# A two-layer encoder trunk on one core: the first weight matrix loaded raw from ScalarE's queue and split on the engines, and two low parts of the first quad computed on VectorE

## The chip, the cores and the metric

The kernel runs on one core of a Trainium2 chip. The metric is the time of one execution on the device, in microseconds (us). The engines are named as in the profile: PE is TensorE (PEld its weight load), DVE is VectorE, ACT is ScalarE, POOL is GpSimd, SP is SyncE. SP, ACT and POOL can issue DMA transfers; SP's and ACT's go through hardware queues, POOL's through a software queue, and all of them share the 16 DMA engines of the core.

## What is computed

Two layers of a bidirectional encoder over 512 tokens of width 1024, in float32. Cut to what matters here, with `P_A` a windowed attention and `P_B` a neighbourhood attention, each followed by a projection:

```python
for l in range(DEPTH):                       # DEPTH = 2
    h = rms_norm(x, attn_norm_g[l])
    z = h @ w_in[l]                          # q_a, k_a, v_a, q_b, k_b, v_b, gate_a, gate_b
    x = x + (sigmoid(ga) * P_A(qa, ka, va) + sigmoid(gb) * P_B(qb, kb, vb)) @ w_out[l]
    h = rms_norm(x, ffn_norm_g[l])
    x = x + (silu(h @ w_gate[l]) * (h @ w_up[l])) @ w_down[l]    # hidden width 2816
```

## The kernel before

**Products in two parts.** A float32 operand is written as a high part, which is the value rounded to the type float32r, and a low part, which is the rest. A product is three matmuls that add into one PSUM bank: high by high, high by low, low by high. So every operand needs both parts before its product can be finished. `mm` (line 619) is one matmul; `UNIT` (line 420) is the planner's time for three.

**Weights.** `slab` (line 442) plans one piece of a weight matrix, at most 128 x 1024 per part; `w_load` (line 503) and `w_low` (line 512) bring it in. The high part is a POOL transfer that rounds on its way. The low part takes two steps: ACT writes minus the high part into the buffer, and a second POOL transfer adds the float32 weights from memory onto it. So a slab is read from memory twice, and ACT's step waits for the first landing and the second transfer for ACT. A slab's two steps fall due `LEAD_H` = 23 and `LEAD_L` = 15 us of planned matmul time ahead of its use; where they fall due before the first matmul, they are issued at the first `tick`.

**The start.** `x_load` (line 641) brings in the input in eight chunks of 128 columns (256 KB each) on SP's queue. SP also issues the identity matrix and the two norm gains, between the first and the second chunk. POOL issues the high parts of the first three slabs and then nine loads of small tables. ACT runs one tiny copy, `warm`, first of all. Then `token_matmul` (line 816) computes the first 512 columns of `z`: four PSUM banks (one for 128 tokens each), eight chunks of the contraction, and so 4 x 3 = 12 matmuls a chunk, 96 in all. A slab holds two chunks of the weights. While it runs, `start` (line 1068) prepares the chunks of x: four PE transposes into one bank, on ACT the high part times the gain, on DVE a copy of the transposed chunk to `xT`, then on DVE the low part, on ACT the square, on DVE the running sum of squares (`acc`). The first half of this (`second` false) and the second half are issued apart, two chunks ahead of their use: chunks 0 and 1 ahead of the first matmul, and chunk k + 2 in the midst of chunk k and its neighbour. Once all squares are added, `Norm.chain` (line 772) has PE sum them over the partitions (the matmuls `at<-ones`), and DVE makes the reciprocal root.

**The feed-forward part.** Its first 256 hidden columns are plain pairs (`pair_matmul`, line 797). The other 2560 are five quads of 512. For a quad the matrix is cut into four blocks and Strassen-like sums of blocks are multiplied: seven products, in the order `ORDER` = (1, 5, 6, 2, 7, 3, 4). `Quad` (line 537) loads the blocks a11, a12, a21, a22 as float32 from SP's queue, and for each product makes the sum on DVE, in place in the blocks (`high`, line 559), the high part on ACT, and the low part (`low`, line 575). In all quads but the first of each layer's `w_gate`, the low part is one DVE subtraction. For that first quad `by_transfer` is true (line 491): `low_by_transfer` (line 532) has ACT write minus the high part, and a POOL transfer from SBUF to SBUF adds the source block onto it. The sums for products 6 and 3 overwrite blocks from which such a transfer reads: product 6 writes a11, the source of product 1; product 3 writes a12, the source of product 2. DVE must wait there for the transfer to have landed. `chain_x` (line 1360) makes the same seven operands from x, and `m_step` (line 1459) multiplies. After product 1, ACT copies its bank to a second one (`seed`, line 1479), onto which products 6, 7 and 4 add.

**The order of the work.** Each engine works in the order in which its instructions were issued. Steps with a due time come from a list (`at_pos`, `tick`); the others are chains (generators), which a planner steps when its own model of the engines' clocks says that their inputs are ready. A dry pass makes these choices and also places all buffers in two arenas by their lives; the second pass follows it. So a change in one place can shift choices and places elsewhere.

Of the kernel before, what the change touches and what calls it, by code (L numbers as in the profile page):

```python
# [19 lines left out]
P = 128  # L20
# [193 lines left out]
def trunk(ctx: ExitStack, tc: tile.TileContext, a: dict, out: bass.AP, lay: Layout):  # L214
# [285 lines left out]

    highs, lows, used = {}, {}, [0]

    def w_load(i):

        if i not in highs:
            n1, n2, src = plan[i]
            highs[i] = buf([n1, n2], F32R)
            for at, ap in src:
                n = ap.shape[1]
                GQ.dma_start(highs[i][:, :, at : at + n], ap.rearrange("(k p) n -> p k n", p=P))  # L510
# [26 lines left out]
    class Quad:  # L537
# [37 lines left out]
        def low(self, m):  # L575
            src, h = self.parts[m]
            lo = buf([4, 256], F32R)
            if self.by_transfer:
                low_by_transfer(lo, src, h)
            else:  # L580
                V.tensor_tensor(lo, src, h.bitcast(F32), ALU.subtract)
            self.parts[m] = h, lo
# [50 lines left out]
    G.memset(vec2, 0.0)  # L633
    G.memset(ones, 1.0)
    G.memset(magic, 0x5F3759DF)
    warm = cp.tile([P, 2], F32, tag="warm", name="warm")
    A.copy(warm, ones)
    xv = a["x"].rearrange("o (b p) d -> p (o b) d", p=P)
    xin = []

    def x_load(c):
        t = act().rearrange("p (b n) -> p b n", b=NB)
        Q.dma_start(t, xv[:, :, P * c : P * c + P])
        xin.append(t)


    x_load(0)
    Q.dma_start(ident, a["consts"][:, :P])
    for i, n in enumerate(("attn_norm_g", "ffn_norm_g")):
        Q.dma_start(vec[16 * i : 16 * i + 16], a[n].rearrange("l (k p) -> (l k) p", p=P))  # L650
    w_load(0)
    for c in range(1, KD):
        x_load(c)
        if c in (3, 5):
            w_load((0, 3, 5).index(c))
    GQ.dma_start(cst[:, P:], a["consts"][:, P:])
    for i, n in enumerate(("q_norm_b", "k_norm_b")):
        for h in range(2):
# [7 lines left out]
        GQ.dma_start(gqa[:, i], a[n].rearrange("l d -> (l d)").unsqueeze(0).to_broadcast([P, DEPTH * HD]))  # L666
    snk = cp.tile([P, DEPTH, 8], F32, tag="snk", name="snk")
    GQ.dma_start(snk, a["sink_a"].rearrange("l h -> (l h)").unsqueeze(0).to_broadcast([P, DEPTH * 8]))
    ps = at_bank()
    T.transpose(ps[:, :32], vec, ident[:32, :32])  # L670
    V.tensor_copy(vecT, ps[:, :32])
# [144 lines left out]
    def token_matmul(nrm, evac, begin=None):  # L816

        ps = [mm_bank() for _ in range(NB)]
        if begin is not None:
            begin(0, False)  # L820
            w_low(0)
            begin(0, True)
            begin(1, False)
            begin(1, True)
            tick(0.0)
        for k0 in range(0, KD, 2):
            wk = w_take()
# [3 lines left out]
            for i, (b, k) in enumerate(order):  # L831
                t = slice(P * b, P * b + P)
                kk = k0 + k
                hi, lo = wk[k]
                mm(ps[b], nrm.xh[kk][:, t], hi, kk == 0, False)
                mm(ps[b], nrm.xh[kk][:, t], lo, False, False)
                mm(ps[b], nrm.xl[kk][:, t], hi, False, kk == KD - 1)
                tick(UNIT)
                if kk == KD - 1:
                    evac(b, ps[b])  # L840
                if begin is not None and i in (0, 2, 4, 6) and k0 < KD - 2:
                    begin(k0 + 2 + i // 4, i % 4 == 2)
                yield UNIT


# [219 lines left out]

    norms = {}

    def start(nrm, k, second):

        if not second:  # L1070
            ps = at_bank()
            for b in range(NB):
                T.transpose(ps[:, P * b : P * b + P], xin[k][:, b, :], ident)
            A.activation(held(nrm.xh[k]), by_columns(ps), AF.Copy, scale=gain(0, k))
            V.tensor_copy(held(xT[k]), by_columns(ps))
            return
        V.scalar_tensor_tensor(nrm.xl[k], xT[k], gain(0, k), nrm.xh[k].bitcast(F32), ALU.mult, ALU.subtract)
        sq = act()
        A.activation(sq, xT[k], AF.Square)
# [512 lines left out]
```

## Time and profile before

| What | us |
|---|---|
| median of 3 runs | 1482.7 |
| the three runs | 1484.63, 1482.7, 1477.24 |
| the profiled execution's own time | 1478.58 |
| its span, first to last instruction | 1476.8 |
| PE busy in it | 1405.2 |
| DVE, ACT, POOL busy | 908.5, 713.9, 368.6 |

The profiled execution took 1478.58 us and its span is 1476.8, so 1.8 us lie outside the span. All positions below are us from the span's start. In a timeline a row is a group of neighbouring instructions of one kind: where it starts, how long the group lasts, engine, operation, output and inputs by their names in the program, shape, count, and in brackets the idle time of the engine ahead of it with what ended it. Almost all instructions carry line 308, which is the helper that records them, so they are told apart by names: `arena` is any buffer in SBUF, `at` and `mm` are PSUM banks. A wait row reads: who waited, for whom, us in all, how often, the longest.

### The profile page before, as it was taken

The numbers are of one execution on the slowest core, as the hardware profiler recorded it, in microseconds if no ns is written. First come the engines' busy times: TensorE is split into PE (matmuls) and PEld (weight loads), VectorE is DVE, ScalarE is ACT, GpSimd is POOL, SyncE is SP. The second block draws the span as 40 slices with busy tenths as digits, with TensorE's granted clock in tenths as the row PEclk, the third lists the DMA queues.
The fourth block names the chain that finished last, engine by engine and source line by source line (L and its number), as shares of the span: only waits on it lengthen the run. The fifth ranks groups of instructions, "written<-read, shape, count | busy, mean of one in ns | idle before, by whom it ended". The sixth has DMA issues, their size and how long they took to land.

```text
span 1476.8 us, 21019 instructions
## 1 busy us (share of the span) xinstructions
PE 1405.2 (95%) x8074; PEld 1230.7 (83%) x8074; DVE 908.5 (62%) x1743; ACT 713.9 (48%) x1200; POOL 368.6 (25%) x374
## 2 busy tenths in 40 slices
PE   5999989999969999999999999999997999999998
PEld 4778878888869999999987887788886899999997
DVE  3876768543747565575647868673437575575653
ACT  3476657543544343433545775574345444343431
POOL 4533222234221110201353322123332211101111
PEclk9999999999989999999999999899999899999999
DMA  9877778899975745645798679669997754836455
GB/s 228 164 145 137 145 128 150 153 191 241 174 150 119 174 115 143 158 100 117 154 189 168 125 132 158 124 122 183 209 242 130 160 124 122 190 83 168 115 100 114
DMA packets 211427, 223.18 MB, mean 151 GB/s; under 512 B 25964, under 2 KB 179744, under 8 KB 211328
## 3 DMA queue, kind: packets, MB, share of 16 engines
q0 software_dynamic: 159920, 167.23, 61.1%
q1 hardware_dynamic: 51408, 54.62, 13.3%
q8 instruction: 63, 1.03, 0.3%
q14 instruction: 36, 0.29, 0.1%
HBM read 207.13 MB, written 2.10 MB: 142 GB/s over the span
## 4 chain that ended last, share of the span: by engine, by line
PE 69%; DMA 9%; DVE 9%; issue 7%; ACT 4%; POOL 2%; DVEq 0%; POOLq 0%; ACTq 0%; SPq 0%
PE mm L308 50%; PE at L308 19%; DVE arena L308 6%; ACT arena L308 4%; DMA arena<-arena 3%; DMA arena<-in_w_out 2%; DVE sm L308 2%; POOL arena L308 2%; DMA arena<-in_w_gate 1%; DMA arena<-in_w_up 1%; DMA arena<-in_rel_bias_b 1%; DMA vec<-in_q_norm_b 1%; DMA arena<-in_w_in 0%; ACT L308 0%; DVE hf L308 0%
## 5 line engine op out<-in xcount | busy, mean ns | idle before, releaser
L308 PE MATMUL mm<-arena 128*128 128x512 f32 (+1 forms) x5568 | 1127.9, 358 | 32.0 <-ACT mm L308 24.9
L308 PEld LDWEIGHTS mm<-arena 128*128 128x128 f32 x5568 | 910.1, 191 | 161.7 <-ACT mm L308 25.3
L308 PE MATMUL at<-arena 128*128 128x256 f32 (+2 forms) x1952 | 309.4, 299 | 15.1 <-DMA arena<-arena 12.3
L308 ACT ACTIVATE arena<-arena 128x1024 fp32r<-128x1024 f32 (+3 forms) x280 | 235.9, 865 | 176.9 <-DMA arena<-in_w_down 62.2
L308 ACT CAST arena<-arena 128x1024 fp32r<-128x1024 f32 (+2 forms) x250 | 211.7, 864 | 224.0 <-DVE arena L308 219.5
L308 PEld LDWEIGHTS at<-arena 128*128 128x128 f32 x1952 | 268.7, 193 | 38.7 <-DMA arena<-arena 11.9
L308 DVE TENSOR_TENSOR arena<-arena,arena 128x1024 fp32r<-128x1024 f32 (+2 forms) x236 | 228.3, 981 | 57.3 <-ACT arena L308 57.1
L308 POOL DMA_DIRECT2D arena<-in_w_in x168 | 168.4, 1367 | 368.3 <-ACT arena L308 367.9
L308 DVE TENSOR_TENSOR arena<-arena,mm 128x512 f32<-128x512 f32 x144 | 98.8, 686 | 255.9 <-PE mm L308 255.8
L308 POOL DMA_DIRECT2D arena<-in_w_down x96 | 98.2, 1210 | 503.2 <-ACT arena L308 388.4
L308 DVE TENSOR_TENSOR arena<-arena 128x1024 f32<-128x1024 f32 (+3 forms) x196 | 158.8, 824 | 19.2 <-DMA arena<-arena 14.1
L308 DVE TENSOR_TENSOR arena<-at,arena 128x384 fp32r<-128x384 f32 (+4 forms) x206 | 114.1, 562 | 52.7 <-ACT arena L308 45.9
L308 ACT CAST arena<-at 128x384 fp32r<-128x384 f32 (+2 forms) x164 | 74.4, 459 | 117.5 <-PE at L308 105.1
L308 PE MATMUL at<-cst,arena 128*128 128x128 f32 x504 | 87.4, 280 | 11.8 <-DVE arena L308 7.9
L308 PEld LDWEIGHTS at<-cst,arena 128*128 128x128 f32 x504 | 64.5, 143 | 30.5 <-DVE arena L308 10.9
L308 ACT ACTIVATE arena<-arena,negm 128x256 f32<-128x256 f32 (+1 forms) x128 | 71.6, 561 | 13.1 <-DVE negm L308 12.7
L308 DVE TENSOR_TENSOR arena<-mm,arena 128x512 f32<-128x512 f32 x72 | 49.3, 687 | 45.8 <-PE mm L308 45.7
L308 ACT COPY arena<-at 64x512 f32<-64x512 f32 (+1 forms) x60 | 34.8, 581 | 64.8 <-PE at L308 64.3
L308 POOL DMA_DIRECT2D arena<-in_w_out x32 | 35.2, 1292 | 54.5 <-ACT arena L308 54.5
L308 DVE CUSTOM_DVE_ANT_0 arena<-at,arena 128x256 f32<-128x256 f32 (+1 forms) x64 | 31.0, 486 | 28.7 <-PE at L308 28.4
L308 DVE CUSTOM_DVE_ANT_0 arena<-at,cst,nsnk 128x256 f32<-128x256 f32 (+1 forms) x64 | 34.3, 546 | 16.3 <-PE at L308 15.9
L308 DVE TENSOR_SCALAR arena<-arena,sm 128x384 f32<-128x384 f32 (+1 forms) x97 | 34.0, 405 | 1.1
(70 smaller groups left out, 444.2 us busy)
## 6 DMA issues: line engine op xcount, KB each, us to landing
arena<-in_w_in POOLq DMA_DIRECT2D x104, 512.0 KB, 7.1
arena<-in_w_down POOLq DMA_DIRECT2D x80, 512.0 KB, 6.8
arena<-in_w_gate SPq DMA_DIRECT2D x20, 1024.0 KB, 6.7
arena<-in_w_up SPq DMA_DIRECT2D x20, 1024.0 KB, 5.2
arena<-in_w_in POOLq DMA_DIRECT2D x64, 256.0 KB, 6.2
arena<-in_w_out POOLq DMA_DIRECT2D x32, 512.0 KB, 8.0
arena<-in_w_proj_a POOLq DMA_DIRECT2D x16, 512.0 KB, 8.8
arena<-in_w_proj_b POOLq DMA_DIRECT2D x16, 512.0 KB, 6.5
```

The costliest lines, as they stand in the source:

```text
L308: f(*args, **kw)
```

## The change

At the start, x and the first matrix (the four slabs of the first 512 columns) come in another way. `first_load` loads a slab as float32 on ACT's hardware queue, once; the first slab in two transfers of one chunk each. `first_parts` makes the two parts of one chunk on the engines: ACT copies it to the high part (which rounds), DVE subtracts. The two gains move from SP's to ACT's queue, the identity goes ahead of x on SP's queue, and `warm` goes behind ACT's transfers. `start` is no longer in two halves: chunk 0 is prepared ahead of the first matmul, and chunk k + 1 after the first bank's three matmuls of chunk k, so one chunk ahead. The copy to `xT` moves from DVE to ACT. In the first quad of each layer, the low parts of products 1 and 2 become DVE subtractions again.

```diff
+    FIRST = KD // 2
+    raws = []
+
+    def first_load(i):
+
+        n1, n2, ((_, ap),) = plan[i]
+        raws.append(buf([n1, n2]))
+        ap = ap.rearrange("(k p) n -> p k n", p=P)
+        for k in ([slice(0, 1), slice(1, 2)] if i == 0 else [slice(0, 2)]):
+            AQ.dma_start(raws[i][:, k], ap[:, k])
+        highs[i], lows[i] = buf([n1, n2], F32R), buf([n1, n2], F32R)
+
+    def first_parts(k):
+        raw, h, lo = raws[k // 2][:, k % 2], highs[k // 2][:, k % 2], lows[k // 2][:, k % 2]
+        A.copy(h, raw)
+        V.tensor_tensor(lo, raw, h.bitcast(F32), ALU.subtract)
...
-            if self.by_transfer:
+            if self.by_transfer and m not in (1, 2):
                 low_by_transfer(lo, src, h)
             else:
                 V.tensor_tensor(lo, src, h.bitcast(F32), ALU.subtract)
...
-    warm = cp.tile([P, 2], F32, tag="warm", name="warm")
-    A.copy(warm, ones)
...
-    x_load(0)
     Q.dma_start(ident, a["consts"][:, :P])
     for i, n in enumerate(("attn_norm_g", "ffn_norm_g")):
-        Q.dma_start(vec[16 * i : 16 * i + 16], a[n].rearrange("l (k p) -> (l k) p", p=P))
-    w_load(0)
-    for c in range(1, KD):
+        AQ.dma_start(vec[16 * i : 16 * i + 16], a[n].rearrange("l (k p) -> (l k) p", p=P))
+    for c in range(KD):
         x_load(c)
-        if c in (3, 5):
-            w_load((0, 3, 5).index(c))
+        if c % 2 == 0:
+            first_load(c // 2)
...
+    warm = cp.tile([P, 2], F32, tag="warm", name="warm")
+    A.copy(warm, ones)
     ps = at_bank()
     T.transpose(ps[:, :32], vec, ident[:32, :32])
...
         if begin is not None:
-            begin(0, False)
-            w_low(0)
-            begin(0, True)
-            begin(1, False)
-            begin(1, True)
+            begin(0)
             tick(0.0)
...
-                if begin is not None and i in (0, 2, 4, 6) and k0 < KD - 2:
-                    begin(k0 + 2 + i // 4, i % 4 == 2)
+                if begin is not None and b == 0 and kk + 1 < KD:
+                    begin(kk + 1)
...
-    def start(nrm, k, second):
-
-        if not second:
-            ps = at_bank()
-            for b in range(NB):
-                T.transpose(ps[:, P * b : P * b + P], xin[k][:, b, :], ident)
-            A.activation(held(nrm.xh[k]), by_columns(ps), AF.Copy, scale=gain(0, k))
-            V.tensor_copy(held(xT[k]), by_columns(ps))
-            return
+    def start(nrm, k):
+
+        first_parts(k)
+        ps = at_bank()
+        for b in range(NB):
+            T.transpose(ps[:, P * b : P * b + P], xin[k][:, b, :], ident)
+        A.activation(held(nrm.xh[k]), by_columns(ps), AF.Copy, scale=gain(0, k))
+        A.copy(held(xT[k]), by_columns(ps))
         V.scalar_tensor_tensor(nrm.xl[k], xT[k], gain(0, k), nrm.xh[k].bitcast(F32), ALU.mult, ALU.subtract)
         sq = act()
         A.activation(sq, xT[k], AF.Square)
```

## The prediction

> **What bounds the kernel now.** I read the page's first part, then PE's waits, then the timeline around the long ones.
>
> ```profile
> PE 1405.2 (95%) x8074; PEld 1230.7 (83%) x8074; DVE 908.5 (62%) x1743; ACT 713.9 (48%) x1200; POOL 368.6 (25%) x374
> ```
>
> PE is busy for 1405.2 of a span of 1476.8 us, so an edit that removes no matmul can win at most the 71.6 us in which PE stands still. PE's waits say where they are:
>
> ```profile
> PE mm L308 <- ACT mm L308: 24.9, 2, 12.5
> ...
> PE mm L308 <- DMA arena<-in_w_in: 7.1, 1, 7.1
> PE at L308 <- DMA vec<-in_ffn_norm_g: 5.9, 1, 5.9
> PE at L308 <- DMA arena<-in_x: 3.9, 1, 3.9
> ```
>
> Two kinds are large: two waits of about 12.4 us for an ACT copy into a bank, and three at the start, 7.1 + 5.9 + 3.9. The change touches both. First the start, from the timeline:
>
> ```profile
> 7.25 0.64 POOL L308 DMA_DIRECT2D posi<-in_positions  x1 [1.05 <-DMA arena<-in_w_in]
> 7.84 1.56 ACT L308 ACTIVATE arena<-arena 128x1024 fp32r<-128x1024 f32 x2
> 12.79 1.28 POOL L308 DMA_DIRECT2D arena<-in_w_in  x1
> 19.80 1.22 PE L308 MATMUL mm<-arena 128*128 128x512 f32 x2 [7.10 <-DMA arena<-in_w_in]
> 28.84 0.60 PE L308 MATMUL at<-cst,arena 128*128 128x128 f32 x4
> 32.05 0.60 PE L308 MATMUL at<-cst,arena 128*128 128x128 f32 x4
> 45.38 1.02 PE L308 MATMUL at<-ones,arena 128*128 128x1 f32 x8 [2.06 <-DVE arena L308]
> 46.27 3.65 PE L308 MATMUL mm<-arena 128*128 128x512 f32 x15
> ```
>
> ACT has written minus the first high part before 9.4, but POOL issues the accumulating transfer only at 12.79: `posi`, its ninth issue, has waited for the landing of its first, and the rest follow in the same way. The stream of matmuls starts at 19.80. From there a chunk takes 32.05 - 28.84 = 3.2 us, and the 96 matmuls end at 46.27 + 3.65 = 49.9.
>
> Now the other kind, in layer 0:
>
> ```profile
> 404.23 2.35 DVE L308 TENSOR_TENSOR arena<-arena,arena 128x1024 fp32r<-128x1024 f32 x2
> 406.06 5.91 PE L308 MATMUL at<-arena 128*128 128x256 f32 x48
> 408.00 1.28 POOL L308 DMA_DIRECT2D arena<-arena  x1 [10.78 <-ACT arena L308]
> 409.41 1.05 ACT L308 ACTIVATE arena<-arena 128x1024 fp32r<-128x1024 f32 x1
> 413.53 1.22 DVE L308 TENSOR_TENSOR arena<-arena 128x1024 f32<-128x1024 f32 x1 [6.94 <-DMA arena<-arena]
> 414.83 1.04 ACT L308 CAST arena<-arena 128x1024 fp32r<-128x1024 f32 x1 [4.37 <-issue]
> 423.74 0.57 ACT L308 COPY mm<-at 128x512 f32<-128x512 f32 x1
> 424.36 1.01 PE L308 MATMUL mm<-arena 128*128 128x256 f32 x3 [12.39 <-ACT mm L308]
> ```
>
> The 48 matmuls are products 1 and 5 of the first quad. PE then needs `seed`, the copy of product 1's bank, which ACT makes at 423.74, long after product 1 was done. ACT works in order: ahead of `seed` stand casts whose sources DVE makes, and DVE has stood still for 6.94 us at the sum for product 3. That sum overwrites a12, which product 2's transfer, issued at 408.00, still reads. The wait row counts two, one in each layer.
>
> **The quads, step by step.** Product 2's low part becomes a subtraction of 1.22 us on DVE:
>
> ```profile
> L308 DVE TENSOR_TENSOR arena<-arena,arena 128x1024 fp32r<-128x1024 f32 x140 | 170.0, 1221 | 32.4 <-ACT arena L308 32.2
> 382.43 1.06 ACT L308 ACTIVATE arena<-arena 128x1024 fp32r<-128x1024 f32 x1
> 382.60 0.69 DVE L308 TENSOR_TENSOR arena<-arena,mm 128x512 f32<-128x512 f32 x1 [2.03 <-PE mm L308]
> 386.90 1.02 PE L308 MATMUL at<-ones,arena 128*128 128x1 f32 x8 [0.26 <-DVE arena L308]
> ```
>
> DVE is done with its earlier work at 406.6. The subtraction takes it to 407.8, and the sum starts there and not at 413.53: 5.7 us earlier. ACT must follow. It loses one negation (1.05), so its next cast and product 7's steps end near 409.5, when the sum has been done for half a microsecond; the cast of 414.83 then starts 5.3 us earlier. From there to `seed` the two engines hand work to each other, and every step moves along. I take 5.5 us, so the wait falls from 12.4 to about 6.9, twice: **-11.0**. It doesn't vanish, because the 10.2 us from 413.53 to 423.74 hold no other transfer. Products 7, 3 and 4 still go by transfer, and their ACT steps move with the chain; those of 7 and 3 stand ahead of `seed`.
>
> Product 1's subtraction lies elsewhere: beside ACT's negation at 382.43, which goes, DVE gets 1.2 us just where the last sums of x and the squares run. If it is ahead of the sum at 382.60, everything up to the matmul at 386.90, which already waits 0.26 for DVE, comes up to 1.2 later; if behind, nothing. I take the middle, 0.6 a layer: **+1.2**. The ends for the quads are -14 (ACT no hindrance, DVE free) and -5 (half of the shift is lost in ACT's queue, and 1.2 is paid twice).
>
> **The start, step by step.** Four slabs are no longer read twice by POOL: eight of its transfers and four negations of 1.05 us on ACT go. ACT gains seven issues. The trace has no issue on ACT's queue; the nearest rows are SP's:
>
> ```profile
> L308 SPq DMA_DIRECT2D arena<-in_x x8: 425/872/2881, 0.7 to 11.9; - x8
> L308 SPq DMA_DIRECT2D arena<-in_w_gate x20: 367/368/1012, 327.0 to 1345.4; - x20
> vec<-in_attn_norm_g SPq DMA_DIRECT2D x1, 8.0 KB, 3.6
> arena<-in_x SPq DMA_DIRECT2D x8, 256.0 KB, 8.1
> ```
>
> The ends are 0.37 and 2.9 us an issue, so 2.6 to 20 for seven. I take 0.45, 3.2 us in all, since a raw transfer is a weight load like `in_w_gate`'s, and that takes 0.37 for 1024 KB. At 2.9 each ACT would come free only at 21, 14.6 later than I put it below; that end alone makes the whole change -15.8 + 14.6 = -1.2, or 1479, and is the range's upper end. A wait comes on top, if a ninth issue on the hardware queues waits for the first landing, as `posi` does on POOL's: SP and ACT issue 16 together, so ACT's last ones would wait for a gain or an early chunk, issued near 2 and landing 3.6 to 8.1 later. I let ACT come free at 6.4, and put behind it its table load and `warm`:
>
> ```profile
> L308 ACT ACT_TABLE_LOAD x2 | 2.6, 1283 | 0.8 <-PEq L1578 0.7
> L308 ACT COPY warm<-ones 128x2 f32<-128x2 f32 x1 | 0.2, 192 | 0.0
> L308 ACT CAST arena<-arena 128x512 fp32r<-128x512 f32 x76 | 46.7, 619 | 89.0 <-DVE arena L308 89.0
> L308 ACT ACTIVATE arena<-at,vecT 128x512 fp32r<-128x512 f32 x8 | 5.5, 683 | 16.9 <-PE at L308 16.9
> L308 ACT COPY arena<-at 128x512 f32<-128x512 f32 x28 | 16.2, 578 | 49.2 <-PE at L308 49.2
> L308 ACT ACTIVATE arena<-arena 128x512 f32<-128x512 f32 x8 | 5.0, 627 | 3.6 <-DVE arena L308 3.6
> L308 DVE SCALAR_TENSOR_TENSOR arena<-arena,vecT,arena 128x512 fp32r<-128x512 f32 x8 | 6.0, 749 | 0.2
> ```
>
> So ACT is ready at 6.4 + 1.3 + 0.2 = 7.9. Chunk 0's cast and high part (0.62 + 0.68) put the first matmul at 9.2; the copy to `xT` and DVE's low part (0.58 + 0.75) put the third at 10.5. I let the stream start at 10.0, **9.8 us earlier** than at 19.80. But then less is done: at 19.80 one matmul and the transposes of chunks 0 and 1 were behind it, and now only those of chunk 0. That is 0.2 + 0.6 = 0.8, so 9.0 are left. The ends: if the data of chunk 0 lands only 8.1 us after an issue near 2, as the median x transfer did, the stream starts some 2 us later; with ACT free at 4, 2 us earlier.
>
> The loop gives some of it back. A chunk now asks of ACT 0.62 + 0.68 + 0.58 + 0.63 = 2.5 us, where it was 0.68 + 0.63; of DVE as much as before, since a copy of 128x512 goes and a subtraction of 128x512 comes. PE takes 3.2. So ACT has 0.7 spare a chunk, and three negations for later slabs (1.05 each), a table load (1.28) and the two sines must fit in 8 x 0.7 = 5.6: they do, but barely, and a chunk is prepared only one ahead. Transposes to the low part take 0.68 + 0.58 + 0.75 = 2.0 us and some hand-overs, and PE has eleven of a chunk's twelve matmuls in front, at 3.65/15 = 0.24 each 2.6. Each of those five ACT pieces, when it falls in between, is about 0.6 late; so is a piece of DVE's table chain. I charge 3.0, between 0 (all fall in gaps) and 9 (both engines' pieces always in between): **-9.0 + 3.0 = -6.0**, ends -11 and +2 with those of the start. The wait of 2.06 at 45.38 stays, as `acc` and the table chain still share DVE.
>
> DMA bandwidth is no term of its own: the start reads four slabs of 512 KB once less, and what PE needs first is one chunk of x and one of the weights, 256 KB each. The chunk of x now goes behind the identity, one issue (0.4) later.
>
> **Sum.** -11.0 + 1.2 - 6.0 = -15.8. The profiled execution took 1478.6, 4.1 below the median of 1482.7. I count from halfway, 1480.6, which gives **1465**. With one term at its end the time is 1460 to 1473 (the start), or 1461 to 1470 (the quads); the far end of ACT's issues, 1479, lies beyond.
>
> **PE's clock** adds to no term but decides the third rival:
>
> ```profile
> 418.00:424.30 6.30, 0.00 (x0) 0.00 (x0) 5.47 (x7) 4.12 (x6) 1.27 (x1) 0.50 1.00 247
> 424.30:430.40 6.10, 6.04 (x28) 6.04 (x29) 2.25 (x3) 3.03 (x5) 3.20 (x3) 0.50 0.53 131
> 430.40:436.00 5.60, 5.60 (x49) 5.60 (x49) 1.44 (x3) 0.60 (x1) 0.00 (x0) 1.00 1.18 228
> ```
>
> In the wait the granted clock falls to 0.50 and stays there 6.1 us after work resumes: 28 matmuls where 49 fit in 5.6 us, about 3 us lost. The Trainium skill (TensorE: Matmul & The Clock Gate, Part 1) says that an idle window of about 3.4 us halves the clock and a busy one restores it. By that rule a wait of 6.9 still pays, and only one under 3.4 saves the 3 as well. The trace agrees: 0.50 after 12.4 us of standing still, while behind the gap of 2.06 fifteen matmuls take 3.65, as fast as before. I leave the 3 us in the sum's both sides.
>
> **Rivals.**
> 1. **ACT paces the start.** With the pieces above always in front of the high part, and `xT` behind them, the loop pays 9: the quads alone remain, -9.8. Time 1471. For it: 2.5 of 3.2 us on an engine that also blocks in order. Against: the negations are far apart. Chance 0.17.
> 2. **The quads keep their wait,** since something else holds ACT ahead of `seed`; the two subtractions cost their 1.2. Then -6.0 + 1.2 = -4.8, 1476. Also the case that the change doesn't do what it says. Against: the 6.94 ends as the transfer lands 5.5 after 408.00. Chance 0.08.
> 3. **The quads' wait goes wholly,** if with DVE free the planner steps the chains in another order and `seed` moves ahead of the casts. Then -2 x (12.4 + 3) + 1.2 - 6.0 = -35.6, 1445. It decides where the wait gets so short that the clock stays up, as it does over the gap of 2.06. Against: the due times stay. Chance 0.08.
> 4. **Slower: the new layout makes later quads wait.** The raw slabs take room in the float32 arena, and all buffers and choices are planned anew. If a later quad's blocks then find their room held, PE waits as it does here, 12.4 + 3 a quad. One such quad undoes the gain; from two on it decides: 31 - 16 = +15, 1496. For it: the blocks are loaded only once their room is free. Against: the wait rows show no other quad waiting now, and the raw slabs are dead after the start. Chance 0.07.
>
> **Chances.** Forecast 0.55, rivals 0.40, and 0.05 for others spread evenly. A difference of about 0.5% (7.4 us) is what a measurement of this kernel can tell from no change, so faster means under 1475.3. Forecast 0.53, rival 1 0.14, rival 2 0.03, rival 3 0.08 and a rest: 0.80 faster. Slower: rival 4 and a little, 0.07. Same: 0.13. The range from 1452 to 1479 leaves out rivals 3 and 4 and tails of 0.05.
>
> **What would show it.** The stream of 128x512 matmuls should start near 10 and its 96 end near 43.9, with waits for ACT or DVE of some 5 us in all. The DVE wait for `arena<-arena` should lose its 7 us; the two PE waits for ACT's bank copy should be near 7 each, with the clock still at 0.50 behind them. Ten transfers `arena<-arena` on POOL, not 14. It is wrong if the first matmul comes after 15, if the chunks take over 4 us, if the wait for the bank copy is above 11 or below 4, or if any other quad waits.

## The result, and the profile after

| | before | after |
|---|---|---|
| median, us (lowest to highest, runs) | 1482.09 (1477.24 to 1484.63, 4) | 1460.84 (1459.94 to 1462.77, 4) |
| the profiled execution, us | 1478.58 | 1459.94 |
| its span, us | 1476.8 | 1458.1 |

The ratio of the times is 0.9858, with a 95% interval of 0.9836 to 0.9881: 21 us faster, where 15.8 were forecast. (The time before has one run more than in the forecast.) The page's first part, after:

```profile
PE 1405.2 (96%) x8074; PEld 1229.1 (84%) x8074; DVE 912.7 (63%) x1747; ACT 714.5 (49%) x1208; POOL 354.5 (24%) x362
```

PE's busy time is the same to a tenth, so on balance all of the gain is time in which PE no longer stands still. Where it stands now, from the waits of PE (us in all, times, the longest):

```profile
PE at L308 <- DVE arena L308: 13.0, 18, 2.3
...
PE mm L308 <- ACT mm L308: 10.0, 2, 5.0
PE mm L308 <- ACT arena L308: 6.7, 2, 6.4
PE at L308 <- DMA vec<-in_ffn_norm_g: 4.1, 1, 4.1
PE at L308 <- DVE rstd L308: 1.3, 1, 1.3
```

The two waits for ACT's bank copy went from 24.9 to 10.0. The waits of the start, which were 7.1 + 5.9 + 3.9, are now 6.4 + 4.1. Two things are new or longer: a wait of 1.3 for the reciprocal root of the first norm, and a wait of 2.3 for DVE, which comes later. The start, in the timeline of after:

```profile
1.66 7.42 ACTq L308 DMA_DIRECT2D arena<-in_w_in  x5
...
9.11 1.28 ACT L308 ACT_TABLE_LOAD   x1 [9.11 <-DMA arena<-in_w_in]
...
10.50 0.61 ACT L308 CAST arena<-arena 128x512 fp32r<-128x512 f32 x1
...
11.76 2.06 PE L308 MATMUL mm<-arena 128*128 128x512 f32 x3 [6.35 <-ACT arena L308]
```

The stream of matmuls starts at 11.76, where it was 19.80. ACT's five issues for the weights take from 1.66 to 9.08, and what ended ACT's idle time is a landing of `in_w_in`: ACT could not issue its last ones before earlier transfers had landed. PE around the end of the first product and the first norm:

```profile
36.10 3.00 PE L308 MATMUL mm<-arena 128*128 128x512 f32 x12
39.08 1.02 PE L308 MATMUL at<-ones,arena 128*128 128x1 f32 x8
39.96 2.35 PE L308 MATMUL mm<-arena 128*128 128x512 f32 x9
43.65 0.62 PE L308 MATMUL at<-cst,rstd 128*128 128x128 f32 x4 [1.35 <-DVE rstd L308]
```

The 96 matmuls end at 39.96 + 2.35 = 42.3, where it was 49.9. The wait of 2.06 ahead of the sum of squares is gone, and 1.35 now stands a little later, ahead of the root's use. Now the first quad in layer 0, after:

```profile
403.21 5.91 PE L308 MATMUL at<-arena 128*128 128x256 f32 x48
404.33 1.23 DVE L308 TENSOR_TENSOR arena<-arena,arena 128x1024 fp32r<-128x1024 f32 x1 [0.87 <-ACT arena L308]
405.47 2.35 DVE L308 TENSOR_TENSOR arena<-arena 128x1024 f32<-128x1024 f32 x2
...
406.77 2.13 ACT L308 CAST arena<-arena 128x1024 fp32r<-128x1024 f32 x2 [1.52 <-DVE arena L308]
...
413.52 0.57 ACT L308 COPY mm<-at 128x512 f32<-128x512 f32 x1
...
414.14 4.78 PE L308 MATMUL mm<-arena 128*128 128x256 f32 x24 [5.02 <-ACT mm L308]
```

DVE goes from its subtraction at 404.33 straight into two sums; the 6.94 us for which it waited there for a transfer are gone. The copy comes 4.4 us after the 48 matmuls end (413.52 - 409.12), where it came 11.8 after (423.74 - 411.97). On POOL ten transfers of the kind `arena<-arena` are left, of 14:

```profile
L308 POOL DMA_DIRECT2D arena<-arena x10 | 11.9, 1189 | 51.9 <-ACT arena L308 48.3 <-DVE sm L308 3.6
```

The places of some landmarks on PE, before and after, show where the time came from (the start of a row of each kernel's timeline, or its end where the table says so; "gained" is the difference so far):

| Landmark on PE | before | after | gained so far |
|---|---|---|---|
| first norm's root used | 49.92 | 43.65 | 6.3 |
| sum of squares ahead of the feed-forward, layer 0 | 386.90 | 382.45 | 4.5 |
| products 1 and 5 of the first quad end | 411.97 | 409.12 | 2.9 |
| PE goes on after the bank copy | 424.36 | 414.14 | 10.2 |
| sum of squares ahead of the feed-forward, layer 1 | 1110.25 | 1098.51 | 11.7 |
| PE goes on after the bank copy, layer 1 | 1147.95 | 1130.20 | 17.8 |
| last group on PE | 1471.98 | 1453.61 | 18.4 |

So the start gave 6.3, the bank copies 7.3 to 7.5 each, and ahead of the feed-forward of layer 0 about 3.4 was lost again, between the first and the third row. That loss was not in the forecast. Its place in after:

```profile
382.45 1.02 PE L308 MATMUL at<-ones,arena 128*128 128x1 f32 x8 [2.26 <-DVE arena L308]
383.33 5.28 PE L308 MATMUL mm<-arena 128*128 128x512 f32 x15
```

PE stood 2.26 us ahead of the sum of squares, where it had stood 0.26 before. The 15 matmuls behind it took 3.67 at the same place before, and 5.28 here. These 1.6 us come back at the bank copy, as the experiments show below; the longer wait does not. In the table by stretches (us, then busy us of PE, PEld, DVE, ACT and POOL; the last three columns are PE's clock, DMA share and GB/s) the clock shows why the matmuls took longer:

```profile
382.40:387.20 4.80, 4.75 (x18) 3.96 (x19) 4.25 (x17) 2.10 (x2) 2.13 (x2) 0.64 0.75 113
...
414.10:417.90 3.80, 3.76 (x17) 3.76 (x18) 0.31 (x1) 2.90 (x4) 2.29 (x3) 0.50 1.03 287
417.90:424.00 6.10, 6.10 (x53) 6.10 (x52) 2.96 (x3) 1.54 (x2) 0.94 (x2) 1.00 1.25 209
```

In the stretch with the 2.26 and the 15 matmuls behind it the granted clock is 0.64 on the mean. Behind the bank copy it stays at 0.50 for 3.8 us now, where it was 6.1.

### The profile page after: what moved, and what is told of

It is laid out like the page before. It is cut to its first block, busy times and chain, and to the rows that moved or that the text cites. A ratio compares the mean times of both kernels' runs of the same rounds, so it can differ in the third digit from the quotient of the medians.

```text
span 1458.1 us, 21020 instructions
## 1 busy us (share of the span) xinstructions
PE 1405.2 (96%) x8074; PEld 1229.1 (84%) x8074; DVE 912.7 (63%) x1747; ACT 714.5 (49%) x1208; POOL 354.5 (24%) x362
## 4 chain that ended last, share of the span: by engine, by line
PE 77%; DVE 9%; DMA 6%; ACT 4%; issue 3%; POOL 1%; ACTq 0%; DVEq 0%; SPq 0%; POOLq 0%
PE mm L308 59%; PE at L308 19%; DVE arena L308 7%; ACT arena L308 4%; DMA arena<-arena 2%; DVE sm L308 2%; DMA arena<-in_w_gate 1%; DMA arena<-in_w_in 1%; DMA arena<-in_w_up 1%; DMA arena<-in_rel_bias_b 1%; POOL arena L308 1%; ACT L308 0%; ACTq L308 0%; DVE hf L308 0%; ACT mm L308 0%
## 5 line engine op out<-in xcount | busy, mean ns | idle before, releaser
L308 ACT CAST arena<-arena 128x1024 fp32r<-128x1024 f32 (+2 forms) x258 | 216.7, 856 | 224.3 <-DVE arena L308 220.5
L308 ACT ACTIVATE arena<-arena 128x1024 fp32r<-128x1024 f32 (+3 forms) x272 | 227.9, 859 | 175.9 <-DMA arena<-in_w_down 63.8
L308 DVE TENSOR_TENSOR arena<-arena,arena 128x1024 fp32r<-128x1024 f32 (+2 forms) x248 | 238.5, 975 | 69.7 <-ACT arena L308 69.5
L308 POOL DMA_DIRECT2D arena<-in_w_in x160 | 159.4, 1382 | 373.1 <-ACT arena L308 363.5
L308 ACT COPY arena<-at 128x512 f32<-128x512 f32 (+1 forms) x68 | 39.5, 581 | 64.2 <-PE at L308 63.6
L308 DVE CUSTOM_DVE_ANT_0 arena<-at,arena 128x256 f32<-128x256 f32 (+1 forms) x64 | 30.8, 485 | 27.1 <-PE at L308 26.6
```

The source lines that it names most:

```text
L308: f(*args, **kw)
```

## The experiments

Each kernel is told by its edit against the changed kernel, or against the one that it says. Medians are in us; the kernel before, run beside them on the same chips, had medians of 1481.0 to 1483.8.

| Kernel | median (lowest to highest, runs) | ratio to before [95%] |
|---|---|---|
| the start alone | 1476.3 (1471.9 to 1480.8, 10) | 0.9967 [0.9947, 0.9987] |
| the two low parts alone | 1467.7 (1462.5 to 1471.2, 4) | 0.9901 [0.9871, 0.9931] |
| start and product 2 | 1459.8 (1457.0 to 1466.8, 6) | 0.9858 [0.9833, 0.9882] |
| start and product 1 | 1473.0 (1471.3 to 1474.4, 4) | 0.9944 [0.9927, 0.9962] |
| raw slabs from SP | 1456.1 (1455.1 to 1461.9, 5) | 0.9830 [0.9809, 0.9852] |
| ... and splits put off | 1460.2 (1456.2 to 1467.4, 4) | 0.9849 [0.9825, 0.9873] |
| ... and slabs' low parts put off | 1453.7 (1450.0 to 1454.8, 4) | 0.9810 [0.9790, 0.9831] |
| ... and bank copy first | 1455.5 (1454.8 to 1463.0, 4) | 0.9825 [0.9781, 0.9869] |
| ... or quad 26 ahead | 1454.5 (1452.5 to 1455.6, 4) | 0.9806 [0.9761, 0.9850] |
| ... or quad 22 ahead | 1449.6 (1446.5 to 1453.3, 4) | 0.9775 [0.9735, 0.9815] |
| warming copy first | 1457.4 (1 run) | |
| `xT` copy on DVE | 1463.2 (1 run) | |

**The start alone.** The first quad's low parts go by transfer as before:

```diff
-            if self.by_transfer and m not in (1, 2):
+            if self.by_transfer:
```

> The start's part alone: all low parts of the first quad go by transfer, as before the change. Theory: the two parts of the change add up, and the start is worth the 6.4 us by which the trace of after is ahead just before the feed-forward part of layer 0 (386.64 against 380.19). So 1482.1 - 6.4 = 1475.7 us, first 128x512 matmul at 11.8, and the two waits of PE for ACT's bank copy back at 12.4 each. Rival: the shorter waits at the quads come from the earlier start or the new plan and not from the low parts; then the waits stay near 5 here and the time is near 1463.

It came out at 1476.3, 5 us under the kernel before, and the two waits for the bank copy were 11.1 and 11.2, a little under the 12.4 expected.

**The two low parts alone.** The kernel before, with the edit of the line above and nothing else.

> The quads' part alone: the start as before, the low parts of products 1 and 2 of the first quad on DVE. Theory: the rest of the gain, 21.3 - 6.4 = 14.9, so 1467 us; waits for the bank copy near 5 each; PE waits 2 us for DVE ahead of the sum of squares in layer 0 and 1 in layer 1, as in after. Rival, as for the run above: waits of 12.4 here and a time near 1480.

1467.7, some 14 us under. PE's waits in it keep the 7.3 of the start, as before, and the bank copies' fall. The waits ahead of the sums of squares were 0.59 and 1.33, where I had expected 2 and 1.

```profile
PE mm L308 <- ACT mm L308: 11.5, 2, 6.4
PE mm L308 <- DMA arena<-in_w_in: 7.3, 1, 7.3
```

5 and 14 make 19 of the 21 us, so the two parts add up within what the intervals allow.

**Start and product 2.** Product 1's low part goes back to its transfer, product 2's stays on DVE:

```diff
-            if self.by_transfer and m not in (1, 2):
+            if self.by_transfer and m != 2:
```

> After, with product 1's low part back on the transfer; product 2's stays on DVE. Theory: product 2's subtraction alone frees the sum for product 3, and product 1's only delays the sums of x and of squares. In after, PE waits 2.26 and 1.43 there (0.26 and 0.29 before) and the clock is halved for 3.4 us behind it, which costs about 1.6 and 1.5 more; all of that goes: 2.0 + 1.6 + 1.1 + 1.5 = 6.2, so 1454.6 us. Rival: both subtractions are needed, since product 6's sum then waits for product 1's transfer and DVE passes the delay on; then the waits for the bank copy grow to 7 or more and the time is 1461 or above.

This theory fell. The time is that of the whole change (1459.8), the waits ahead of the sums of squares were still 1.92 and 1.18, and those for the bank copy 5.0 and 5.1. Product 1's subtraction costs nothing that these times can tell, and it brings nothing.

**Start and product 1**, the other half: `m != 1` in the same line.

> The whole change, except that product 2's low part goes by the accumulating transfer as before, so that of the two low parts only product 1's is made on VectorE. My theory: the long wait for ScalarE's bank copy hung on product 2's transfer alone, so both waits come back to 11 to 12.5 us (5.0 with the whole change), VectorE again stands still some 7 us for a transfer in the first quad, and the time is the changed kernel's 1461 + 2 x (6.5 + 1) = 1476. The rival, that ScalarE was late because it had two negations of 1.05 us in the first quad, whichever products they were for, would halve the gain: waits near 8.5 and some 1468.

The waits came back to 11.0 and 12.3, and DVE stands still again for product 2's transfer:

```profile
412.02 1.23 DVE L308 TENSOR_TENSOR arena<-arena 128x1024 f32<-128x1024 f32 x1 [6.94 <-DMA arena<-arena]
```

The stand of 6.94 is to the hundredth that of the kernel before. The time of 1473.0 is 3 below what I expected, but the waits are nowhere near the rival's 8.5. With the run before it, this shows that the gain of the quads is product 2's, as far as the intervals can tell.

**Raw slabs from SP.** All raw slabs but the first are issued from SP's queue, between the chunks of x, so that ACT has four issues and not seven:

```diff
-            AQ.dma_start(raws[i][:, k], ap[:, k])
+            (Q if i else AQ).dma_start(raws[i][:, k], ap[:, k])
```

> After, with slabs 1 to 3 of the first matrix issued raw on SP's queue between the x chunks, and only slab 0 on ACT's. Theory: in after the first chunk's data is there at about 6.5, but ACT is held to 9.1 by its last issue, which waits for an earlier landing, and then loads its table; so without these issues the first matmul comes at 8.0 and not 11.8, the 96 end 3.7 earlier, and the time is 1457. Rival: the transfers are the pace; in one queue x and the weights come later, the chunks wait for data, and the time is 1461 or more.

As the theory had it: 1456.1, and the start, in its timeline, without a held issue on ACT:

```profile
1.66 1.09 ACTq L308 DMA_DIRECT2D arena<-in_w_in  x2
...
2.78 1.28 ACT L308 ACT_TABLE_LOAD   x1 [2.78 <-issue]
...
6.54 0.62 ACT L308 CAST arena<-arena 128x512 fp32r<-128x512 f32 x1 [2.27 <-DMA arena<-in_w_in]
...
7.80 2.06 PE L308 MATMUL mm<-arena 128*128 128x512 f32 x3 [1.96 <-ACT arena L308]
```

ACT is done with its issues and `warm` by 4.3 and waits 2.27 for the data. The matmuls start at 7.80, and the 96 end at 38.7, 3.6 earlier than in the changed kernel. The held issues now stand on SP, where no computing waits behind them. The waits for the bank copy are 6.5 and 6.4 here, longer than the changed kernel's 5.0, and those ahead of the sums of squares are 1.92 and 0.37.

**Warming copy first.** In the changed kernel, the two lines of `warm` go back ahead of ACT's issues.

> The whole change, with ScalarE's little warming copy, and so its table load of 1.28 us, ahead of its DMA issues. If ScalarE is held at the start by its seventh issue, which waits for an earlier landing (8.71 us in the changed kernel), the table load then lies in that wait: the first matmul of product size moves from 11.76 to about 10.3, unless the issues, now 1.5 us later, land later by as much. The rival, that the landings and not ScalarE's own queue set the start, leaves the first matmul at 11.5 to 12. The time itself is expected within 2 us of the changed kernel's 1461 either way; the place of the first matmul and of the end of the 96 (42.3 in the changed kernel) is what tells the two apart.

```profile
0.74 1.28 ACT L308 ACT_TABLE_LOAD   x1 [0.74 <-PEq L1588]
...
2.75 7.61 ACTq L308 DMA_DIRECT2D arena<-in_w_in  x4
10.41 0.62 ACT L308 CAST arena<-arena 128x512 fp32r<-128x512 f32 x1 [8.18 <-DMA arena<-in_x]
```

The table load costs nothing at 0.74, but ACT's last issue then ends at 10.36, not at 9.08: the held issues came later by what the table load had taken. The first matmul is at 11.67 and the 96 end at 42.5, so nothing is won. The single time, 1457.4, is 3.5 below the changed kernel's; its start does not explain that, and one run cannot tell more.

**`xT` copy on DVE**, as before the change, in the changed kernel (`V.tensor_copy` for `A.copy` in `start`). It asks whether ACT paces the start.

> The whole change, but with the copy of the turned chunk to its kept place on VectorE, as before the change, so that a chunk of the start asks 0.58 us less of ScalarE and 0.69 more of VectorE. My rival that ScalarE paces the start would have it pay 3 us or more here: with the first matmul again near 11.8, the 96 matmuls would end before 40 (42.3 in the changed kernel). Theory: the stops inside the chunk loop are 1.1 us in all there, so ScalarE doesn't pace it, and no more than that can be won: the 96 end between 41.2 and 43, the time within 2 us of 1461.

Nothing was won, and my bounds were missed on the other side: from nearly the same first matmul (11.38) the 96 end at 45.4, 3 us later. The stretch of the chunk loop, in this kernel and in the changed one (us, then busy us of PE, PEld, DVE, ACT and POOL):

```profile
11.40:43.00 31.60, 27.47 (x124) 20.60 (x124) 27.21 (x65) 18.36 (x29) 5.87 (x7) 1.00 0.72 170
```

```profile
11.80:39.90 28.10, 26.93 (x124) 20.67 (x124) 21.93 (x58) 22.17 (x37) 5.91 (x7) 1.00 0.80 189
```

With the copy on DVE, DVE is busy for 27.2 of 31.6 us and PE's waits, near 4 us in all, are mostly for it; with the copy on ACT both stand near 22 of 28.1. So the move of that copy to ACT is worth 3 us in the trace. The forecast had seen it leave DVE, but gave it no price. Since DVE took over the load, this run cannot say by itself whether ACT paces the changed kernel; that its stops inside the loop are 1.1 us in all is read from the changed kernel's own rows.

**Splits put off.** On top of the raw slabs from SP, the splits of the two gated products are put off by 3.5 and 4.5 us, so that the bank copy would come ahead of them on ACT:

```diff
-            split(gt[j], h, lo)
+            at_pos(pos[0] + 3.5 + j, lambda: split(gt[j], h, lo))
```

> The raw slabs issued from SyncE (1456.1, with bank-copy waits of 6.5 and 6.4 us), and the split of the two gated products into high and low parts, which stands on ScalarE's queue ahead of the bank copy, put off by 3.5 and 4.5 us of matmul time, so that the copy comes first. My theory: what is left of the wait is ScalarE's order, two casts of 0.62 us that wait for VectorE's products, and no longer any transfer. Then both waits fall to 2 to 4 us, the clock recovers sooner, and the time is 1456 - 2 x 4 = about 1448, between 1445 and 1451. The rival, that VectorE is full from the reciprocal root to the copy and the casts only take the order that it gives, leaves the waits at 5 to 6.5, since the quad's own casts wait for VectorE as well: 1454 to 1456.

The theory fell, and the rival was too kind: the waits grew from 6.5 and 6.4 to 8.5 and 7.1. (The profiled execution is the slowest of the four, 1467.4, so its waits are compared here and not its time.) The row on ACT ahead of the copy:

```profile
414.38 1.04 ACT L308 CAST arena<-arena 128x1024 fp32r<-128x1024 f32 x1 [2.14 <-DVE arena L308]
415.45 0.57 ACT L308 COPY mm<-at 128x512 f32<-128x512 f32 x1
```

Where one cast had gone, the planner put another one ahead of the copy, and that waits for DVE as well (a step of 1.22 that DVE starts only at 413.07).

**Slabs' low parts put off.** On top of the raw slabs from SP, the low parts of the eight slabs ahead of the first quad come 4 us of planned time later (the added arguments go through to `slab`'s `later_h` and `later_l`). It asks for the cause of the wait ahead of the sum of squares.

```diff
-        plan_pair(a["w_gate"][l], 0, KD)
-        plan_pair(a["w_up"][l], 0, KD)
+        plan_pair(a["w_gate"][l], 0, KD, 0, 4.0)
+        plan_pair(a["w_up"][l], 0, KD, 0, 4.0)
```

> The raw slabs issued from SyncE, and the low parts of the eight slabs ahead of the first quad (first columns of the gate and up matrices) put off by 4 us of matmul time. My theory for the wait ahead of the sum of squares before the feed-forward (1.9 and 0.4 us in the kernel with raw slabs from SyncE): ScalarE stands some 3 us at the negation for one of these slabs, whose high part has not landed, and the last squares come behind it. Then that stand goes to 1 us or less and the two waits to under 0.5, worth some 2 us and the half clock behind the first of them, and the time is 1452 to 1455. The rival: the wait is set by VectorE's own chain of sums, and the waits stay at 1 to 2 us and the time at 1456.

The changed kernel on ACT, ahead of the sum of squares at 382.45:

```profile
375.93 1.06 ACT L308 ACTIVATE arena<-arena 128x1024 fp32r<-128x1024 f32 x1 [3.14 <-DMA arena<-in_w_up]
...
379.81 0.72 ACT L308 ACTIVATE arena<-arena,vecT 128x512 fp32r<-128x512 f32 x1 [0.74 <-DVE arena L308]
380.44 0.61 ACT L308 ACTIVATE arena<-arena 128x512 f32<-128x512 f32 x1
```

ACT had the same kind of stand in the kernel before:

```profile
380.40 1.06 ACT L308 ACTIVATE arena<-arena 128x1024 fp32r<-128x1024 f32 x1 [2.87 <-DMA arena<-in_w_up]
```

In both kernels the sum of squares comes 6.5 us after this stand has ended (386.90 - 380.40 and 382.45 - 375.93). But the stand's end moved by 4.5, and PE's earlier work by 6.3 with the start, so PE now gets there first and waits. And the kernel of this experiment, with PE's rows:

```profile
371.99 0.73 ACT L308 ACTIVATE arena<-arena,vecT 128x512 fp32r<-128x512 f32 x1 [1.47 <-DVE arena L308]
372.62 0.62 ACT L308 ACTIVATE arena<-arena 128x512 f32<-128x512 f32 x1
```

```profile
375.14 0.95 PE L308 MATMUL at<-ones,arena 128*128 128x1 f32 x8
375.95 3.71 PE L308 MATMUL mm<-arena 128*128 128x512 f32 x15
```

The last square ends at 373.2, two us ahead of its use, and PE waits in neither layer. So the wait ahead of the sum of squares came from ACT's stand behind a slab whose high part had not landed, with the last squares queued behind it; a stand for an earlier slab (3.7 us) is still there and does no harm. The time is 2.4 lower, which the two intervals do not separate; the rows do.

**Bank copy first.** On top of that, the copy is issued straight behind product 1's matmuls, and both splits are put off until they lie behind it.

```diff
+            if m == 1:
+                seed()
+                return
             soon({
-                1: seed,
...
-            split(gt[j], h, lo)
+            at_pos(pos[0] + (10.0, 4.5)[j], lambda: split(gt[j], h, lo))
```

> The fastest so far (raw slabs from SyncE, low parts of the gate and up slabs put off by 4 us: 1453.7, bank-copy waits of 6.2 and 6.2 us), with the bank copy issued as soon as product 1's matmuls are, and both splits of the gated products put off until they stand behind it on ScalarE's queue. In the run where I put them off before, one of the two was still ahead and a cast for x's product 4, which waits for VectorE, had come in as well; the waits grew to 8.5 and 7.1. Theory, now that VectorE's time is the limit and not ScalarE's order: the casts that stay ahead wait for VectorE too, and the waits are 5 to 8 us, the time 1452 to 1457. The rival, that it was the one split left ahead, lets the waits fall to 2 to 4 and the time to 1446 to 1449.

The waits were 7.7 and 7.7, the time 1455.5 (the profiled execution, 1463.0, is the slowest of the four). With both splits gone, three casts of 128x1024 stand ahead of the copy at 413.65; the last of them starts at 412.58, after 1.99 us in which ACT waits for DVE. So putting off the splits is not enough, because the casts that take their place wait for DVE as well. A copy ahead of all these casts, or on another engine, was not run, so ACT's order is not ruled out as part of what is left of the wait.

**Quad 26 and 22 ahead.** Against the kernel with the slabs' low parts put off, the first quad's steps fall due 26 or 22 us of matmul time early, not 18 (`early = 26.0` and `22.0` in the planner), so that some of DVE's sums lie ahead of the reciprocal root.

> The fastest so far, with the first quad's parts begun 8 us of matmul time earlier (26 instead of 18 ahead), so that some of its sums of 1.22 us on VectorE lie ahead of the reciprocal root, where VectorE has gaps. Theory: from the root to the bank copy VectorE is full, 27 us of work without a gap over 0.9 us, so each sum or subtraction that leaves this stretch takes 1.2 off both waits: three or four leave, the waits fall from 6.2 to 1.5 to 3, and with the shorter half clock the time is 1444 to 1449. The rivals: the transfers of products 7, 3 and 4 that start earlier hold a sum as product 2's did (waits back to 6 or more, 1453 to 1460); or the moved sums delay the squares, and the wait ahead of the sum of squares grows by what the other loses (1452 to 1455).

> As the kernel with 26, with the first quad's parts begun 22 us of matmul time ahead instead of 18. Theory: one or two of the sums of 1.22 us leave the full stretch of VectorE, the waits fall from 6.2 to 3.5 to 5, and the time is 1449 to 1452, between that of 18 (1453.7) and that of 26. The rival, that VectorE's load isn't what the wait hangs on, leaves waits near 6 and 1453 to 1455.

DVE from the root to the bank copy, in the changed kernel and in the one with 22:

```profile
386.40:413.50 27.10, 22.73 (x123) 19.53 (x122) 24.41 (x30) 16.76 (x18) 4.98 (x5) 0.94 0.52 82
```

```profile
387.20:408.60 21.40, 18.45 (x105) 15.70 (x103) 18.51 (x25) 15.16 (x17) 6.80 (x6) 1.00 0.90 160
```

DVE is busy for 24.4 of 27.1 us in the changed kernel: 90%, with no gap over 0.9. With 22 it has five instructions of 1.2 fewer in the stretch, and PE's rows read:

```profile
395.92 5.29 PE L308 MATMUL mm<-arena 128*128 128x512 f32 x22 [1.30 <-DMA arena<-in_w_up]
...
409.23 4.82 PE L308 MATMUL mm<-arena 128*128 128x256 f32 x24 [2.27 <-ACT mm L308]
```

The waits for the copy are 2.27 and 2.33, lower than I had expected of it, and the time of 1449.6 is as expected. A wait of 1.3 for a weight slab is new in each layer. So most of what was left of the wait hangs on DVE's load in that stretch. With 26 the wait of layer 0 falls to 0.9, but that of layer 1 only to 4.9, and the time is no better than with 18, since a new wait stands earlier, for a weight slab (in layer 1 it is 1.74):

```profile
390.58 1.65 PE L308 MATMUL mm<-arena 128*128 128x512 f32 x3 [4.78 <-DMA arena<-in_w_up]
```

None of my rivals had that one. That the earlier loads and transfers of the quad push this slab's landing back is only argued; no run took them apart. The kernel with 22 has the lowest median of all. It is 2.25% under the kernel before [1.85%, 2.65%], and the changed one 1.42% [1.19%, 1.64%], so it beats that one. From the one with 18 (1.90% [1.69%, 2.10%]) only the rows separate it.

**From the sum of squares to the bank copy.** This is no run of its own but a reading of those above in which no split is put off and the quad does not start earlier. PE has the same work in all of them between the sum of squares ahead of the feed-forward and the bank copy. The table gives how long the 15 matmuls behind the sum took, and how far behind the sum's start PE goes on after the copy. (The two kernels with one run agree: 31.3 to 31.7.)

| Kernel | 15 matmuls, layer 0 | sum to copy, layer 0 | 15 matmuls, layer 1 | sum to copy, layer 1 |
|---|---|---|---|---|
| before | 3.67 | 37.5 | 3.69 | 37.7 |
| the start alone | 5.27 | 37.8 | 6.37 | 39.5 |
| start and product 1 | 5.28 | 37.7 | 3.67 | 37.4 |
| changed | 5.28 | 31.7 | 5.28 | 31.7 |
| start and product 2 | 5.25 | 31.7 | 5.21 | 31.7 |
| the two low parts alone | 3.67 | 31.5 | 5.27 | 31.7 |
| raw slabs from SP | 3.67 | 31.6 | 3.69 | 31.5 |
| ... and slabs' low parts put off | 3.71 | 31.2 | 3.71 | 31.3 |

For raw slabs from SP it is this row, less the 377.89 at which its sum of squares starts:

```profile
409.45 5.43 PE L308 MATMUL mm<-arena 128*128 128x256 f32 x24 [6.49 <-ACT mm L308]
```

With product 2's low part on DVE the stretch is 31.2 to 31.7, whether the 15 matmuls run at full or at half clock; without, it is 37.4 to 37.8, but for 39.5 once, where the sum's own eight matmuls were slow too (1.53 us for 1.02). So, but for that one case, the 1.6 us that half the clock costs there is not lost: PE waits that much less for the copy. This is why the wait reads 5.0 in the changed kernel and 6.5 with raw slabs from SP, and 11.1 with the start alone where it was 12.4 before.

## Why the prediction came out as it did

The mechanism was right, and so were the side and the range (1452 to 1479; 1460.8 measured). By its steps:

- **The quads' wait: right in cause, and within 0.8 us in size.** The waits fell from 12.4 and 12.5 to 5.0 each, 14.9 in all, where 11.0 were forecast. But about 1.6 of each is only PE coming later, by the half clock behind the sum of squares. Counted from the sum of squares to the copy, the stretch went from 37.46 to 31.69 and from 37.70 to 31.69: 5.8 and 6.0 shorter, 11.8 in all. Inside it two sizes were wrong and nearly cancel, which is luck. The sum for product 3 came 3.6 earlier and not 5.7 (413.53 - 386.90 = 26.6 behind the sum of squares before, 405.47 - 382.45 = 23.0 now), because two more subtractions, not one, and a wait of 0.87 for ACT now lie ahead of it. And "from there to `seed` the two engines hand work to each other, and every step moves along" failed on the good side: from its cast to the copy it is now 413.52 - 406.77 = 6.8, where it was 423.74 - 414.83 = 8.9. In the rows of after, two sums lie back to back at 405.47 and two casts at 406.77; before, the second such cast came only at 419.83, 5.0 behind the first.
- **Product 1's subtraction.** Charged with 1.2, and measured as nothing that the medians can tell. Without it the waits ahead of the sums of squares are 0.3 shorter each.
- **The start: -6.0 forecast, -6.3 in the trace, and 5 measured by itself,** but by terms that cancel. ACT came free at 9.1 and not at 6.4, so the stream started at 11.8 and not at 10.0. That ACT's last issues would be held until an earlier landing was said; that the landing would be a raw slab's at 8.7 was only in the range ("8.1 after an issue near 2"). The loop charge of 3.0 was too high: the stops in the loop are 0.25 + 0.38 + 0.49 = 1.1. So the stream starts 8.0 earlier and not 9.8; from there to the end of the 96 it takes 0.4 longer (30.55 against 30.1) and not 3.8; and 1.35 is paid at the root: 6.3. ACT, with its 22 of 28 us, stops PE for 0.38 of that time, and DVE would be the limit if the copy to `xT` had stayed there.
- **"The wait of 2.06 at 45.38 stays"** failed: it went, and 1.35 came back at the root.
- **The wait ahead of the feed-forward's sum of squares** (0.26 to 2.26 in layer 0, 0.29 to 1.43 in layer 1) stood in no step and in no rival. It takes back 3.1 us. The clock behind it costs the 15 matmuls 1.6 in each layer (5.28 us, where 3.67 is full speed), but the wait for the copy is shorter by as much. I first laid it to product 1's subtraction, which the run without that refuted; the run with the slabs' low parts put off shows its cause.
- **The clock: "I leave the 3 us in the sum's both sides."** It changed: the half clock behind the bank copy lasts 3.8 us and not 6.1, worth 1.0 in layer 0 and 0.7 in layer 1 by PE's rows behind the copies. The prediction had it from the Trainium skill (TensorE: Matmul & The Clock Gate, Part 1) that an idle window of about 3.4 us halves the clock, and took from this that only a wait under 3.4 keeps it up. The rows bear that out in one direction only. After 5.0 the clock is at 0.50; but it also fell behind the 2.26 here, and with quad 22 ahead behind 2.27 (24 matmuls in 4.82), though not behind 2.33 in its layer 1 (3.34).
- **The base.** The forecast, 1464.8 unrounded, lies 4.0 above the median of 1460.8. The two profiled executions are 18.6 apart and not 15.8, which is 2.8 of it. On the one side stand the quads' 0.8, product 1's 1.2, the start's 0.3 and the clock's 1.7, 4.0 together, on the other the 3.1 ahead of the two sums of squares. That leaves 1.9 unexplained; PE's rows put 1.6 of it between the bank copy of layer 0 and the sum of squares of layer 1, and no run looked for its cause. The other 1.1 lie between the executions that were summed and the medians, whose runs lie up to 7 apart.

Of the rivals, the first (ACT paces the start), the second (the quads keep their wait) and the fourth (later quads wait) did not occur: no other quad waits in the rows above. The third (the wait goes wholly) would have needed DVE's load to move, not only product 2's transfer: 22 ahead gets within 2.3 us of it.

## What to carry to other kernels

When a step that an engine waited for goes away, look for what shares that engine's stretch up to the waiter: here the wait did not vanish, since DVE was 90% busy from the root to the copy, and moving five of its steps ahead did more than the two reorderings on ACT that were tried. A wait can also shrink only because the waiter comes later, so count from the landmark where the work behind it begins. Put issues that may be held onto a queue whose engine has nothing behind them. And a step moved earlier gains until its own transfers meet another's: 22 us ahead had shorter waits than 18 and the lower median, and 26 gave it back.

## What the runs showed of the hardware

**Held issues on ACT.** An issue on ACT's queue takes 0.4 to 0.5 us by itself, but the five of the changed kernel took 7.4, and ACT's computing stood behind them. With two of them only, they took 1.09. Which transfer's landing frees which issue was read from one semaphore event and not varied by itself, beyond the run in which the table load ahead of them moved the whole row by 1.28.

**The clock does not follow the length of a wait alone.** Two waits at the same place, in the kernel with the start alone and in that with raw slabs from SP:

```profile
381.80 1.02 PE L308 MATMUL at<-ones,arena 128*128 128x1 f32 x8 [1.09 <-DVE arena L308]
382.68 5.27 PE L308 MATMUL mm<-arena 128*128 128x512 f32 x15
```

```profile
377.89 1.02 PE L308 MATMUL at<-ones,arena 128*128 128x1 f32 x8 [1.92 <-DVE arena L308]
378.78 3.67 PE L308 MATMUL mm<-arena 128*128 128x512 f32 x15
```

Behind 1.09 us the 15 matmuls take 5.27, at half the clock; behind 1.92 they take 3.67, at the full one. The Trainium skill (TensorE: Matmul & The Clock Gate, Part 1) says that the window in which activity is judged runs freely, so that the same kernel can meet it at different phases. That fits both rows, but no run here moved a wait against the window alone. An estimate of what a short wait costs should therefore hold both: nothing, or about 1.6 us on top; and where PE soon has to wait for another engine anyway, as it does here for the bank copy, even the 1.6 comes back.
